# The second column half of a projection, token block by token block, from weights kept in dead tiles

## The chip, the core and the metric

The kernel runs on one core of a Trainium2 chip. The metric is the device time of one execution in microseconds. Shown are the median of several runs, and one profiled execution with its own time.

## The reference

One sequence of 512 tokens with 1024 features passes through two blocks of two layers. In the first block a layer ends twice in a layer norm, each over a sum with a projection:

```python
x = layer_norm(ALPHA * x + mix, ln1_g[l], ln1_b[l])   # mix = merged @ w_o[l]
ffn = conv_ffn(x, ffn_w_up[l], ffn_conv_w[l], ffn_conv_b[l], ffn_w_down[l])
x = layer_norm(ALPHA * x + ffn, ln2_g[l], ln2_b[l])
```

In the second block each layer has three sublayers: a mixer (RG-LRU in the first layer, RWKV-7 in the second), a cross attention into 256 memory tokens, and an MLP of 4096 with a squared ReLU. Each of them reads an RMS norm of `x`, and each result is normed before it is added:

```python
x = x + rms_norm_2(t, g[1])                            # t = mixer(hn) @ w_out (+ b_out)
c = mem_cross_attention(rms_norm_2(x, g[2]), mem_n, c_w_q[i], c_w_kv[i], c_w_o[i])
x = x + rms_norm_2(c, g[3])
m = sqrelu_mlp(rms_norm_2(x, g[4]), m_w_up[i], m_w_down[i])
x = x + rms_norm_2(m, g[5])
```

All of it is float32.

## The kernel before

The 512 tokens are four blocks of 128, t0 to t3. A float32 product is made of three matmuls in a rounded type: each operand is split into a high and a low part, and high x high, high x low and low x high are added in PSUM (`mm3`, and L347 to L349 in `nmm`). A weight unit is 128 x 1024. `W` (L277 to L285) brings it in: a transfer on SP's queue into `wst` (two buffers, L280), the high part by ACT into `whi` (four buffers, L283), the low part by POOL into `wlo` (three buffers, L284). Behind a transposed input of 1024 features a projection to 1024 columns has two column halves of 512, with four units each, and each unit serves two of the eight feature chunks.

A projection whose result has tokens on the partitions goes through `nmm`: four PSUM banks, one for each token block (three under the name `mm`, one under `av`), and for each unit 6 matmuls per block. The argument `tail` says how many of the last units are run block by block: 1 in the first column half; 3 in the second, so that the first unit is run for all blocks, and then t0 has its other 18 matmuls, then t1, and so on. When a block's last matmul is done, `evac` reads its bank and the norm of that block begins; `skew` holds the norms as generators, so that their stages are emitted staggered. The program's order is not the final one: a scheduler in the compiler orders each engine's instructions by what they wait for, and it mixes the blocks.

Nine projections are followed by a norm over their rows. In the order of time: wo0 (`attention`'s end in the first block), wn0 (the FFN's down projection), wo1, wn1, wlo (the RG-LRU's output, with a bias), wco0 (cross attention), wmd0 (MLP down), wco1 and wmd1; RWKV's output has another form and is untouched. In the FFN and the MLP the down projection is summed over groups of chunks; the last group is the one before the norm. The FFN's last group has six chunks, three units for each half, with a tail of two. The MLP's 32 chunks go in groups of 6, 6, 6, 6, 6 and 2, so its last group has one unit for each half.

Behind the last matmul of a block in the second block of the network come (`out_proj`, `post`, `pre_norm`): ACT's square with its sum (L906), VectorE's product with the norm's row (L963; for wlo and the MLP POOL's, L967 and L1154), an inverse root in small VectorE steps (L374 to L380, L911), the pair of L945 that adds the result to `x`, then the next norm: squares (L906), products with its row by POOL and VectorE (L922), the inverse root, and the diagonal `dg` (L926). The transposes at L931 are matmuls of `work` with `dg`, eight for each token block, and ACT (L295) and VectorE (L297) split their result into `xTh` and `xTl`. In the first block of the network `ln_fin` does the same with a layer norm (L414 to L442) and `to_T` transposes (L391). The next stage starts with `lead`: the first output tiles are computed for tokens 0 to 255, as soon as two blocks are transposed, and then for the others. The weights of `lead` are loaded ahead and split by ACT and POOL.

## Time and profile before

| | before |
|---|---|
| median of 3 runs | 3947.04 us (3946.8 to 3949.09) |
| profiled execution | 3947.95 us, span 3946.2 us |
| mean granted clock of TensorE | 0.951 |
| TensorE (PE) busy | 3724.7 us, 94% |
| VectorE (DVE) busy | 1740.0 us, 44% |
| POOL busy | 1639.7 us, 42% |
| ACT busy | 1505.6 us, 38% |
| chain that ended last | PE 81%, DVE 11%, DMA 3% |

The span is what the profile covers; the time of the execution is 1.75 us longer. PE means TensorE's matmuls and PEld its weight loads, which run beside them. A clock of 1.00 is the higher of TensorE's two levels. A busy share is a mean over stages with different limits, so that an engine at 44% can still be what a stage waits for.

### The profile page before, as it was taken

To read this page: it belongs to the slowest core of one execution; us is meant where nothing else is said; L and a number is where in the kernel's file an instruction comes from. 1 tells how busy PE (TensorE), PEld (TensorE's weight loads), DVE (VectorE), ACT (ScalarE), POOL (GpSimd) and SP (SyncE) were. 2 spreads that over 40 slices of the span, in tenths; PEclk is the share of its full clock that TensorE was granted. 3 is DMA by queue.
4 is the path that set the end of the run, shared out by engine and by line. 5 is a ranking of instruction groups with operands and counts; after the bars stand their busy time and mean duration, and the time that the engine had idled before them with its cause. 6 is when DMAs were issued, how large, how long until landed. Compare 5 with 4: busy or idle time off the path is not lost.

```text
span 3946.2 us, 48388 instructions
## 1 busy us (share of the span) xinstructions
PE 3724.7 (94%) x18540; PEld 2992.9 (76%) x18540; DVE 1740.0 (44%) x3587; ACT 1505.6 (38%) x2653; POOL 1639.7 (42%) x876
## 2 busy tenths in 40 slices
PE   8999998999999999989997888999799899798998
PEld 8766777888886677778886777888676677687886
DVE  4553354433545424453437645221468545534113
ACT  4433333433344334333334634332354334343322
POOL 4421436444452233444444562344434322434444
PEclk9999999999999999999998998999899658899999
DMA  5311323333342122232321321222223311322222
GB/s 188 115 54 48 92 61 126 91 99 97 125 150 70 59 72 70 91 111 93 100 92 59 101 102 64 86 96 92 97 75 96 70 39 49 121 80 84 98 91 86
DMA packets 148952, 354.10 MB, mean 90 GB/s; under 512 B 50080, under 2 KB 60864, under 8 KB 148464
## 3 DMA queue, kind: packets, MB, share of 16 engines
q1 hardware_dynamic: 148448, 350.18, 27.4%
q8 instruction: 146, 2.39, 0.2%
q0 software_dynamic: 272, 0.82, 0.1%
q14 instruction: 86, 0.70, 0.1%
HBM read 332.56 MB, written 18.38 MB: 89 GB/s over the span
## 4 chain that ended last, share of the span: by engine, by line
PE 81%; DVE 11%; DMA 3%; ACT 2%; POOL 2%; issue 1%; SPq 0%; DVEq 0%; POOLq 0%; ACTq 0%
PE mm L289 13%; PE mm L291 13%; PE mm L290 13%; PE mm L1626 3%; PE mm L348 3%; PE mm L347 3%; PE mm L349 3%; PE mm L1144 2%; PE mm L1146 2%; PE mm L1145 2%; PE sc L778 2%; PE mm L862 2%; PE mm L861 2%; PE mm L860 2%; PE av L616 1%
## 5 line engine op out<-in xcount | busy, mean ns | idle before, releaser
L284 POOL TENSOR_TENSOR wlo<-wst,whi 128x1024 fp32r<-128x1024 f32 (+1 forms) x556 | 1340.5, 2414 | 1912.2 <-PE mm L291 971.2
L283 ACT ACTIVATE whi<-wst 128x1024 fp32r<-128x1024 f32 (+1 forms) x556 | 582.8, 1048 | 1134.0 <-DMA wst<-in_wmd 143.3
L289 PE MATMUL mm<-xTh,whi 128*128 128x512 f32 (+1 forms) x2208 | 834.2, 380 | 10.6 <-ACT whi L283 10.3
L290 PE MATMUL mm<-xTl,whi 128*128 128x512 f32 (+1 forms) x2208 | 834.5, 379 | 2.3 <-DVE xTl L297 2.1
L291 PE MATMUL mm<-xTh,wlo 128*128 128x512 f32 (+1 forms) x2208 | 833.4, 378 | 0.0
L289 PEld LDWEIGHTS mm<-xTh,whi 128*128 128x128 f32 x2208 | 417.7, 190 | 96.2 <-ACT whi L283 11.7
L291 PEld LDWEIGHTS mm<-xTh,wlo 128*128 128x128 f32 x2208 | 418.2, 190 | 84.3 <-issue 8.7
L290 PEld LDWEIGHTS mm<-xTl,whi 128*128 128x128 f32 x2208 | 418.5, 190 | 83.9 <-issue 7.8
L822 DVE SCALAR_TENSOR_TENSOR fup<-mm,vec,fup 128x511 f32<-128x511 f32 (+1 forms) x176 | 131.6, 748 | 237.5 <-ACT fup L820 234.5
L784 ACT ACTIVATE P<-sc,sm 128x128 f32<-128x128 f32 x192 | 100.7, 525 | 229.5 <-DVE sm L782 229.5
L781 DVE TENSOR_TENSOR sc<-sc,cst 128x128 f32<-128x128 f32 x192 | 56.0, 297 | 277.2 <-PE sc L780 258.5
L1117 DVE TENSOR_TENSOR relu<-relu,mm 128x512 f32<-128x512 f32 x64 | 43.9, 687 | 294.5 <-ACT relu L1116 294.5
L349 PE MATMUL mm<-whi,xTl 128*128 128x512 f32 (+1 forms) x432 | 164.3, 383 | 2.4 <-DVE xTl L297 2.4
L348 PE MATMUL mm<-wlo,xTh 128*128 128x512 f32 (+1 forms) x432 | 165.4, 383 | 0.0
L347 PE MATMUL mm<-whi,xTh 128*128 128x512 f32 (+1 forms) x432 | 161.4, 383 | 2.4 <-ACT zkv L475 1.1
L1144 PE MATMUL mm<-whi,ph 128*128 128x512 f32 x384 | 151.9, 396 | 0.0
L1145 PE MATMUL mm<-wlo,ph 128*128 128x512 f32 x384 | 151.9, 396 | 0.0
L931 PE MATMUL tr<-dg,work 128*128 128x128 f32 x384 | 67.3, 348 | 89.4 <-DVE dg L926 80.0
L1146 PE MATMUL mm<-whi,pl 128*128 128x512 f32 x384 | 150.2, 396 | 0.0
L931 PEld LDWEIGHTS tr<-dg,work 128*128 128x128 f32 x384 | 63.7, 258 | 93.5 <-issue 63.1
L1151 DVE TENSOR_TENSOR work<-work,mm 128x512 f32<-128x512 f32 x60 | 41.2, 687 | 190.1 <-PE mm L1146 190.1
L860 PE MATMUL mm<-whi,hh 128*128 128x512 f32 x264 | 103.6, 392 | 0.0
(554 smaller groups left out, 7184.7 us busy)
## 6 DMA issues: line engine op xcount, KB each, us to landing
wst<-in_wu SPq DMA_DIRECT2D x88, 512.0 KB, 3.6
wst<-in_wmu SPq DMA_DIRECT2D x64, 512.0 KB, 3.6
wst<-in_wmd SPq DMA_DIRECT2D x64, 512.0 KB, 3.6
wst<-in_wg SPq DMA_DIRECT2D x48, 512.0 KB, 3.6
wst<-in_wn SPq DMA_DIRECT2D x44, 512.0 KB, 3.6
wst<-in_wa SPq DMA_DIRECT2D x24, 512.0 KB, 3.6
wst<-in_wb SPq DMA_DIRECT2D x24, 512.0 KB, 3.6
wst<-in_wd SPq DMA_DIRECT2D x24, 512.0 KB, 3.6
```

The lines of the kernel that those rows point to most:

```text
L283: nc.scalar.activation(hi, st, AF.Copy)
L284: nc.gpsimd.tensor_sub(lo, st, hi.bitcast(F32))
L289: mm(out, lh, rh, start=start, stop=False)
L290: mm(out, lh, rl, start=False, stop=False)
L291: return mm(out, ll, rh, start=False, stop=stop)
L347: mm(o, xh, hi[:, s], start=k == 0, stop=False)
L348: mm(o, xh, lo[:, s], start=False, stop=False)
L349: mm(o, xl, hi[:, s], start=False, stop=k == nk - 1)
L860: mm(pss[t], hh[:, ts], wh[:, s], start=j == js[0], stop=False)
L1144: mm(pss[t], hh[:, ts], wh[:, s], start=j == js[0], stop=False)
L1145: mm(pss[t], hh[:, ts], wl[:, s], start=False, stop=False)
L1146: mm(pss[t], hl[:, ts], wh[:, s], start=False, stop=j == js[-1])
```

## The change

In the nine projections the second column half runs one token block after the other: all 24 matmuls of t0 (18 where there are three units), then those of t1, and so on (`tokens`). That needs all units of this half at once. They are loaded during the first half, in turn with its own units (`side` in `nmm`): `W_in` brings a unit through `wst` like `W`, but splits it into tiles that are dead in this stage, under the name `wres`. These are 512 columns wide, so that ACT and POOL have two splits for each unit, except at wco, where two large tiles hold two units each. In the MLP the groups of chunks become 6, 6, 6, 4, 4 and 6, so that its last group has three units for each half. The number of matmuls and of transfers is as before; ACT and POOL have 24 splits more.

```diff
+KEEP = dict(ffn=(["q"] * 4, ["k"] * 2 + ["pt"] * 2, ["tmp"] * 4), mlp=(["q"] * 4, ["k"] * 4, ["tmp"] * 4))
...
+    def W_in(self, name, u, his, los):
+        nc = self.nc
+        st = self.wp.tile([128, 1024], F32, tag="wst", bufs=2, name="wst")
+        nc.sync.dma_start(st, self.I[name][u])
+        w = 1024 // len(his)
+        for i, (hi, lo) in enumerate(zip(his, los)):
+            s = slice(i * w, i * w + w)
+            nc.scalar.activation(hi, st[:, s], AF.Copy)
+            nc.gpsimd.tensor_sub(lo, st[:, s], hi.bitcast(F32))
+        if len(his) == 2:
+            return list(zip(his, los))
+        return [(his[0][:, i * 512:i * 512 + 512], los[0][:, i * 512:i * 512 + 512]) for i in range(2)]
+
+    def halves(self, tags):
+        a = [self.t([128, 512], tag, {"pt": 9, "tmp": 5}.get(tag, 8), F32R, "wres") for tag in tags]
+        return a[:2], a[2:]
+
+    def tokens(self, xT, units, evac, bank="mm"):
+        mm = self.nc.tensor.matmul
+        pss = self.banks(NT)
+        for t in range(NT):
+            ts = slice(t * 128, t * 128 + 128)
+            for k, (hi, lo) in enumerate(units):
+                xh, xl = xT[k][0][:, ts], xT[k][1][:, ts]
+                mm(pss[t], xh, hi, start=k == 0, stop=False)
+                mm(pss[t], xh, lo, start=False, stop=False)
+                mm(pss[t], xl, hi, start=False, stop=k == len(units) - 1)
+            evac(t, pss[t])
...
         for kp in range(nu):
             units.append(self.W(name, u0 + kp))
+            if kp < len(side):
+                side[kp]()
...
-            self.nmm(f"wo{l}", 4 * cb, self.pairs(mT), evo, tail=1 if cb == 0 else 3)
+        self.two_pass(f"wo{l}", self.pairs(mT), evo, [lambda i=i: self.halves(("k" if i < 2 else "pt",) * 4) for i in range(4)])
...
+    def two_pass(self, name, yT, evac, tiles):
+        units = []
+
+        def load(i):
+            units.extend(self.W_in(name, 4 + i, *tiles[i]()))
+        self.nmm(name, 0, yT, lambda t, ps: evac(0, t, ps), side=[lambda i=i: load(i) for i in range(4)])
+        self.tokens(yT, units, lambda t, ps: evac(1, t, ps))
...
-            for cb, ev in todo:
-                self.nmm(name, 4 * cb, yT, ev, tail=1 if cb == 0 else 3)
+            self.two_pass(name, yT, ev, tiles)
...
-        groups = [range(6 * a, min(32, 6 * a + 6)) for a in range(6)]
+        ends = [6, 12, 18, 22, 26, 32]
+        groups = [range(a, b) for a, b in zip([0] + ends, ends)]
...
+                if fin and cb == 1:
+                    self.tokens([hs[j] for j in js], kept, evac)
+                    continue
+                kept = []
+
+                def keep(a):
+                    kept.extend(self.W_in(f"wmd{i}", 16 + js[0] // 2 + a, *self.halves(KEEP["mlp"][a])))
+                self.nmm(f"wmd{i}", cb * 16 + js[0] // 2, [hs[j] for j in js], evac, nk=len(js),
+                         side=[lambda a=a: keep(a) for a in range(nu)] if fin else ())
```

The FFN's last group is written in the same way as the MLP's. In wco the tiles are two of the large ones, in wlo those of the names k, k, pt and q.

The first place where the order moves is TensorE in the second column half of wco0. `mm_18529` to `mm_18531` and `av_18532` are the banks of t0 to t3, `whi_18577` and `wlo_18578` the last unit. Before, near the end of the half:

```order
L347 MATMUL av_18532<-whi_18565,ph_18190 128x512
L348 MATMUL av_18532<-wlo_18566,ph_18190 128x512
L348 MATMUL mm_18529<-wlo_18578,ph_18360 128x512
L349 MATMUL mm_18529<-whi_18577,pl_18361 128x512
L347 MATMUL mm_18529<-whi_18577,ph_18371 128x512
L348 MATMUL mm_18529<-wlo_18578,ph_18371 128x512
L349 MATMUL mm_18529<-whi_18577,pl_18372 128x512
L348 MATMUL mm_18530<-wlo_18578,ph_18360 128x512
L349 MATMUL mm_18530<-whi_18577,pl_18361 128x512
L347 MATMUL mm_18530<-whi_18577,ph_18371 128x512
L348 MATMUL mm_18530<-wlo_18578,ph_18371 128x512
```

Here t3's bank gets matmuls of the second unit while t0 and t1 still lack most of the last. In the changed kernel (the banks are `mm_18619` to `mm_18621` and `av_18622`, the units lie in the two `wres`), at the passage from t0 to t1:

```order
L316 MATMUL mm_18619<-wres_18544,ph_18432 128x512
L317 MATMUL mm_18619<-wres_18544,pl_18433 128x512
L315 MATMUL mm_18619<-wres_18544,ph_18443 128x512
L316 MATMUL mm_18619<-wres_18544,ph_18443 128x512
L317 MATMUL mm_18619<-wres_18544,pl_18444 128x512
L315 MATMUL mm_18620<-wres_18475,ph_18177 128x512
L316 MATMUL mm_18620<-wres_18475,ph_18177 128x512
L317 MATMUL mm_18620<-wres_18475,pl_18178 128x512
L315 MATMUL mm_18620<-wres_18475,ph_18188 128x512
```

The 24 matmuls of t0 stand one behind the other, then the 24 of t1; behind those of t3 come the transposes of t0, those of t1 and the lead.

The second place is POOL at the same time: the splits of the next stage's weights (wmu, of the MLP's up projection) against the multiplications of the second norm (`work` from `x` and `row`, one for each token block). Before, where `wlo_18893`, `wlo_18899` and `wlo_18905` are the next stage's:

```order
L284 TENSOR_TENSOR wlo_18572<-wst_18569,whi_18571 128x1024
L284 TENSOR_TENSOR wlo_18578<-wst_18575,whi_18577 128x1024
L284 TENSOR_TENSOR wlo_18893<-wst_18890,whi_18892 128x1024
L284 TENSOR_TENSOR wlo_18899<-wst_18896,whi_18898 128x1024
L922 TENSOR_TENSOR work_18377<-x_13033,row_18387 128x512
L922 TENSOR_TENSOR work_18379<-x_13034,row_18387 128x512
L284 TENSOR_TENSOR wlo_18905<-wst_18902,whi_18904 128x1024
L922 TENSOR_TENSOR work_18381<-x_13035,row_18387 128x512
L922 TENSOR_TENSOR work_18383<-x_13036,row_18387 128x512
L284 TENSOR_TENSOR wlo_19079<-wst_19076,whi_19078 128x1024
```

In the changed kernel, where `wlo_18959`, `wlo_18965` and `wlo_18971` are the next stage's:

```order
L297 TENSOR_TENSOR wres_18475<-wst_18510,wres_18475 128x1024
L285 TENSOR_TENSOR wlo_18541<-wst_18538,whi_18540 128x1024
L297 TENSOR_TENSOR wres_18544<-wst_18545,wres_18544 128x1024
L297 TENSOR_TENSOR wres_18544<-wst_18579,wres_18544 128x1024
L285 TENSOR_TENSOR wlo_18576<-wst_18573,whi_18575 128x1024
L285 TENSOR_TENSOR wlo_18959<-wst_18956,whi_18958 128x1024
L285 TENSOR_TENSOR wlo_18965<-wst_18962,whi_18964 128x1024
L285 TENSOR_TENSOR wlo_18971<-wst_18968,whi_18970 128x1024
L959 TENSOR_TENSOR work_18449<-x_13061,row_18459 128x512
L959 TENSOR_TENSOR work_18451<-x_13062,row_18459 128x512
L959 TENSOR_TENSOR work_18453<-x_13063,row_18459 128x512
L959 TENSOR_TENSOR work_18455<-x_13064,row_18459 128x512
```

The kept units' splits stand between those of the first half, and all three splits of the next stage stand ahead of the four multiplications.

## Rows read from the trace of the kernel before

**Rows 1.** The page, busy time, share of the span and instructions of each engine.

```profile
PE 3724.7 (94%) x18540; PEld 2992.9 (76%) x18540; DVE 1740.0 (44%) x3587; ACT 1505.6 (38%) x2653; POOL 1639.7 (42%) x876
```

**Rows 2.** Table of waits, PE: us in total, times, longest.

```profile
PE tr L931 <- DVE dg L926: 80.0, 9, 21.0
```

**Rows 3.** Windows: width, busy (count) of PE, PEld, DVE, ACT, POOL, PEclk, DMA share, GB/s.

```profile
671.85:707.50 35.65, 25.77 (x177) 24.56 (x178) 23.08 (x41) 12.79 (x18) 19.57 (x11) 0.76 0.29 88
1050.10:1066.70 16.60, 12.98 (x65) 10.99 (x63) 16.46 (x44) 6.29 (x10) 10.21 (x11) 0.90 0.40 147
1713.66:1749.00 35.34, 24.99 (x178) 23.93 (x178) 23.15 (x41) 12.80 (x18) 19.59 (x11) 0.81 0.29 104
2095.38:2138.10 42.72, 19.93 (x140) 19.65 (x141) 33.48 (x110) 14.36 (x30) 16.27 (x10) 0.68 0.06 19
2299.16:2342.05 42.89, 28.29 (x209) 27.85 (x210) 29.47 (x83) 15.48 (x33) 18.60 (x10) 0.80 0.26 94
2445.79:2487.70 41.91, 28.77 (x209) 28.24 (x210) 29.72 (x85) 16.56 (x35) 16.29 (x8) 0.80 0.21 70
2824.88:2860.29 35.41, 11.21 (x66) 10.63 (x65) 30.78 (x91) 16.22 (x38) 16.34 (x21) 0.70 0.26 90
3554.05:3594.40 40.35, 27.00 (x209) 26.42 (x210) 28.44 (x85) 16.52 (x35) 15.31 (x8) 0.87 0.16 54
3931.61:3946.20 14.59, 0.00 (x0) 0.00 (x0) 10.31 (x36) 0.86 (x4) 2.64 (x3) 0.60 0.36 144
```

**Rows 4.** Windows, the stretch of wco0 in which TensorE stands still.

```profile
2449.79:2457.11 7.32, 0.00 (x0) 0.03 (x1) 7.32 (x34) 4.34 (x10) 4.39 (x3) 0.50 0.24 87
```

**Rows 5.** Windows, work behind wco0 at full clock, and 128x512 matmuls of wco0.

```profile
2471.17:2487.70 16.53, 16.53 (x142) 16.53 (x142) 5.45 (x7) 5.69 (x9) 4.47 (x2) 1.00 0.07 17
...
2424.00:2436.00 12.00, 12.00 (x53) 9.64 (x52) 1.38 (x2) 3.75 (x5) 6.02 (x3) 1.00 0.32 108
```

**Rows 6.** Timeline of ACT in wco0: start, us, instruction, idle before it.

```profile
2439.81 0.60 ACT L906 ACTIVATE junk<-mm 128x512 f32<-128x512 f32 x1 [6.88 <-PE mm L349]
...
2440.98 0.60 ACT L906 ACTIVATE junk<-mm 128x512 f32<-128x512 f32 x1 [0.48 <-PE mm L349]
```

**Rows 7.** Timeline of DVE in wco0.

```profile
2444.09 4.59 DVE L945 SCALAR_TENSOR_TENSOR x<-work,rsq,x 128x512 f32<-128x512 f32 x2
...
2450.52 1.41 DVE L945 SCALAR_TENSOR_TENSOR x<-work,rsq,x 128x512 f32<-128x512 f32 x2
...
2456.68 0.28 DVE L926 TENSOR_SCALAR dg<-cst,rsq 128x128 f32<-128x128 f32 x1
...
2461.76 0.27 DVE L926 TENSOR_SCALAR dg<-cst,rsq 128x128 f32<-128x128 f32 x1
```

**Rows 8.** Timeline of POOL in wco0.

```profile
2442.98 5.15 POOL L284 TENSOR_TENSOR wlo<-wst,whi 128x1024 fp32r<-128x1024 f32 x2 [8.80 <-PE av L349]
```

**Rows 9.** Timeline of DVE at the kernel's end, the last pair.

```profile
3940.58 1.41 DVE L945 SCALAR_TENSOR_TENSOR x<-work,rsq,x 128x512 f32<-128x512 f32 x2
```

**Rows 10.** The page, groups of the splits, and transfers of a weight unit.

```profile
L284 POOL TENSOR_TENSOR wlo<-wst,whi 128x1024 fp32r<-128x1024 f32 (+1 forms) x556 | 1340.5, 2414 | 1912.2 <-PE mm L291 971.2
L283 ACT ACTIVATE whi<-wst 128x1024 fp32r<-128x1024 f32 (+1 forms) x556 | 582.8, 1048 | 1134.0 <-DMA wst<-in_wmd 143.3
...
wst<-in_wmd SPq DMA_DIRECT2D x64, 512.0 KB, 3.6
```

**Rows 11.** Timeline of SP, the issues of wlo's eight transfers.

```profile
2237.50 37.22 SPq L280 DMA_DIRECT2D wst<-in_wlo  x8
```

**Rows 12.** Timeline of DVE in wn1: t0's last addition, the first diagonal.

```profile
2087.02 0.69 DVE L868 TENSOR_TENSOR x<-x,mm 128x512 f32<-128x512 f32 x1 [6.98 <-PE mm L862]
...
2115.94 0.27 DVE L926 TENSOR_SCALAR dg<-cst,rsq 128x128 f32<-128x128 f32 x1
```

**Rows 13.** Timeline of DVE behind wmd0: the last diagonal.

```profile
2852.98 0.29 DVE L926 TENSOR_SCALAR dg<-cst,rsq 128x128 f32<-128x128 f32 x1
```

**Rows 14.** Windows, a stretch of the RWKV stage.

```profile
3160.00:3220.00 60.00, 56.57 (x337) 43.79 (x336) 32.48 (x90) 27.18 (x75) 26.76 (x48) 0.59 0.17 42
```

More of the change, by code (lines that the diff above doesn't have):

```diff
@@ L873, in down, with keep @@
+                if fin and cb == 1:
+                    self.tokens([hs[j] for j in js], kept, evac)
+                    continue
+                kept = []
+                def keep(i):
+                    kept.extend(self.W_in(f"wn{l}", 11 + js[0] // 2 + i, *self.halves(KEEP["ffn"][i])))
+                self.nmm(f"wn{l}", u0, [hs[j] for j in js], evac, nk=len(js),
+                         side=[lambda i=i: keep(i) for i in range(nu)] if fin else ())
             if fin:
@@ L1103, in cross, with tiles @@
         T2 = self.newT()
-        self.out_proj(f"wco{i}", o, x, post_g, pre_g, T2)
+        hold = []
+        def tiles(i):
+            if i % 2 == 0:
+                hold.append(self.big([128, 2, 2, 1024], name="wres"))
+            a = hold[-1][:, i % 2]
+            return [a[:, 0]], [a[:, 1]]
+        self.out_proj(f"wco{i}", o, x, post_g, pre_g, T2, tiles=[lambda i=i: tiles(i) for i in range(4)])
         return self.pairs(T2)
@@ L1132, in down @@
             for cb in range(2):
-                pss = self.banks(NT)
-                units = [self.W(f"wmd{i}", cb * 16 + js[0] // 2 + a) for a in range(nu)]
-                order = [(t, a) for a in range(nu - 1) for t in range(NT)] + [(t, nu - 1) for t in range(NT)]
-                for t, a in order:
-                    wh, wl = units[a]
-                    ts = slice(t * 128, t * 128 + 128)
-                    for kk in range(2):
-                        j = js[2 * a + kk]
-                        s = slice(kk * 512, kk * 512 + 512)
-                        hh, hl = hs[j]
-                        mm = nc.tensor.matmul
-                        mm(pss[t], hh[:, ts], wh[:, s], start=j == js[0], stop=False)
-                        mm(pss[t], hh[:, ts], wl[:, s], start=False, stop=False)
-                        mm(pss[t], hl[:, ts], wh[:, s], start=False, stop=j == js[-1])
-                    if a == nu - 1:
-                        if gi == 0:
-                            nc.scalar.activation(work[t][cb], pss[t], AF.Copy)
-                        else:
-                            nc.vector.tensor_add(work[t][cb], work[t][cb], pss[t])
-                        if fin:
-                            self.square(work[t][cb], ss[t], cb)
-                            nc.gpsimd.tensor_mul(work[t][cb], work[t][cb], gp[:, cb * 512:cb * 512 + 512])
-                        if fin and cb == 1:
-                            self.skew(fin_row(t))
@@ new lines, in evac @@
+                def evac(t, ps, cb=cb):
+                    if gi == 0:
+                        nc.scalar.activation(work[t][cb], ps, AF.Copy)
+                    else:
+                        nc.vector.tensor_add(work[t][cb], work[t][cb], ps)
+                    if fin:
+                        self.square(work[t][cb], ss[t], cb)
+                        nc.gpsimd.tensor_mul(work[t][cb], work[t][cb], gp[:, cb * 512:cb * 512 + 512])
+                    if fin and cb == 1:
+                        self.skew(fin_row(t))
@@ L1157, in down @@
+                if fin and cb == 1:
+                    self.tokens([hs[j] for j in js], kept, evac)
+                    continue
+                kept = []
+                def keep(a):
+                    kept.extend(self.W_in(f"wmd{i}", 16 + js[0] // 2 + a, *self.halves(KEEP["mlp"][a])))
+                self.nmm(f"wmd{i}", cb * 16 + js[0] // 2, [hs[j] for j in js], evac, nk=len(js),
+                         side=[lambda a=a: keep(a) for a in range(nu)] if fin else ())
             if fin:
@@ L1277, in rglru @@
         T2 = self.newT()
-        self.out_proj("wlo", self.pairs(yT), x, ROW_G + 1, ROW_G + 2, T2, bias=ROW_BOUT)
+        self.out_proj("wlo", self.pairs(yT), x, ROW_G + 1, ROW_G + 2, T2, bias=ROW_BOUT,
+                      tiles=[lambda g=g: self.halves(g) for g in (["k"] * 4, ["k"] * 4, ["pt"] * 4, ["q"] * 4)])
         return self.pairs(T2)
```

93 lines of the change are left out of this document (36 added, 57 removed).

## The prediction

> **What bounds the kernel now.** I read the page first: TensorE is busy 3724.7 of 3946.2 us [rows 1], so the kernel is bound by matmuls and can only shorten where TensorE stands still or runs slowly. The table of waits says where it stands: TensorE's largest wait, 80.0 us in nine times, is that of the transposes at L931 for the diagonal `dg` that VectorE writes last in a norm [rows 2]. The third view is the table of windows, one window for each of the nine places where a projection is followed by a norm: from the end of the projection's last matmul (E below) to the point where the next matmuls run without a stop [rows 3]. The nine windows are 305.5 us together, and TensorE is busy in 178.9 us of them. Besides, the granted clock in them is 0.60 to 0.90, and 0.50 in the stretch of wco0 in which TensorE has nothing to do [rows 4]: of the two levels, 1.2 and 2.4 GHz, that is the lower, so the first transposes behind an idle stretch run at half speed.
>
> What would these windows be if nothing waited? After wco0 the work at full clock is 142 instructions in 16.53 us, 0.1164 us each; a 128x512 matmul goes at 53 in 12.00 us, 0.226 us each [rows 5]. Width less count times 0.1164 is a window's excess: wo0 35.65 - 177 x 0.1164 = 15.0; wo1 14.6; wn1 26.4; wlo 18.6; wco0 17.6; wmd0 27.7; wco1 16.0; wmd1, the kernel's end, 14.6. In wn0 many of the 65 instructions are wider, so there I take the idle 3.6 and a tenth of the busy 12.98 for the clock, 5. The sum is 155: the most that this change can win, were everything behind it free.
>
> Why the wait is so long is seen at wco0. The four token blocks are nearly finished together: ACT's first squares of t0 and t1 start at 2439.81 and 2440.98, when their matmuls are done, 6.0 and 4.8 us ahead of E = 2445.79 [rows 6]. VectorE then serves four blocks at once: the diagonals of t0 and t1 come at 2456.68 and 2461.76, 16.9 and 20.8 us behind those ends [rows 7]. In that time POOL splits weights of the next stage, two in 5.15 us from 2442.98 [rows 8], and VectorE's pair of L945 takes 4.59 us, against 1.41 us a little later [rows 7].
>
> **The change, part by part.** No matmul goes or comes. In the second column half a token block runs its 24 matmuls (18 at wn and wmd) without a break. At 0.226 us that is 5.4 us (4.1), so t0 is finished at E - 16.3, t1 at E - 10.9, t2 at E - 5.4 (E - 12.2, - 8.1, - 4.1). E itself stays where it was if the weights come in time.
>
> *Four places alike (wo0, wo1, wco0, wco1).* t0 is finished 10 us and t1 6 us earlier against E. Their chains keep the same instructions, but two blocks share VectorE where four did. How long one then takes no row shows. The nearest row from below is the kernel's end, where the last block's chain ends 10.4 us behind E, 3941.99 against 3931.61, though without the second norm [rows 9]; from above, 16.9 and 20.8 as now. I take the middle, 13.5 for t0 and 16 for t1. So t0's diagonal is there before E and t1's at E + 5.1, with t0's eight transposes, 0.9 us, to run meanwhile: 4 us stay. TensorE's pause is then too short for most of the loss by clock. The gains are 11.0, 10.6, 13.6 and 12.0, together 47.2. The bounds are 6 each (t1's shift alone, chains as long as now) and the whole excess.
>
> *wlo.* As wco0, with a bias addition more in the chain: 5 us stay. But here the supply costs something. A unit takes its buffer through a transfer (3.6), ACT's split (1.05) and POOL's (2.41) [rows 10], 7.1 us; with two buffers one unit every 3.5 us. The first half now needs eight units, 28 us, where its matmuls take 96 x 0.226 = 21.7. If nothing is loaded ahead, the price is 28 - 21.7 = 6.5 us. wlo's transfers are issued from 2237.50 on [rows 11], and its first matmul runs some 192 x 0.226 = 43 us before E = 2299.16, at 2256: a lead of 18 us, which the two buffers and the three sets of split tiles can't hold in full. I put 4 us of the 6.5. At the other four places of this size the transfers stand in SP's order ahead of the last work of the stage before, which covers them; I cost them at nothing, and 6.5 each if that cover is gone. Gain 18.6 - 9 = 9.6.
>
> *wn0.* 5 to 2: gain 3.
>
> *wn1.* t0's last addition starts at 2087.02, 8.4 us before E = 2095.38, and the first diagonal comes at 2115.94 [rows 12]; VectorE is busy 33.48 of 42.72 us there [rows 3]. So the bounds are 12.2 - 7.7 = 4.5 (t0's earlier end) and VectorE's idle 9.2. I take 7.
>
> *wmd0.* Blocks are now 1.4 us apart, and the next stage needs all four: t3's diagonal comes at 2852.98, 28.1 us behind E, for VectorE is busy 30.78 of 35.41 with all four [rows 3, 13]. In the change t0's chain and most of t1's run before E, and t3 queues behind one block: about 10.4 and one more norm, 14. Gain 14, bounds 4 (half of t0's 8.1 us shift) and 18.
>
> *wmd1.* The last block alone: E + 10.4 becomes about E + 6, and the output's transfer of 4.2 us stays. Gain 4.5, bounds 2 and 6.
>
> *Groups of chunks in the MLP.* There are six groups as before, so as many additions and as many matmuls; the last, of six chunks instead of two, gives the blocks their 18 matmuls. Cost nothing. *Splits:* ACT and POOL get 24 instructions more, each over half a width, beside matmuls. *Order:* the scheduler also moves RWKV steps against each other. There the clock is 0.59 in a stretch with TensorE busy 56.57 of 60 us [rows 14], so that TensorE, not a wait, sets the pace. I count it at nothing; one such stretch at full clock instead of half, or the reverse, is 30 us, and I take that as the bound either way.
>
> **Sum.** 47.2 + 9.6 + 3 + 7 + 14 + 4.5 = 85.3. The profiled execution took 3947.95 us, 0.9 above the median of 3947.04; 3947.95 - 85.3 = 3862.6, less 0.9 is **3862 us**.
>
> **The rule that speaks against it.** VectorE's pair at 4.59 us ran beside POOL's splits, and at 1.41 without them [rows 7, 8]. In the order of the change all three splits for the next stage stand ahead of POOL's four multiplications of the norm; I expect them to run before t0's L945, while t0's matmuls run. If they fall on it instead, each place but the last pays 4.59 - 1.41 = 3.2 us again, up to 8 x 3.2 = 25 us less gain: 3887. The Trainium skill, page SBUF — State Buffer, section Who interferes with whom, says that a VectorE instruction with two SBUF inputs contends with a GpSimd instruction that reads SBUF, and that for the shared ports whoever issues first blocks the other; L945 reads `work` and `x`, so by that rule the new splits would stretch it wherever they overlap, and the time would be that of this case. The trace agrees that the pair is stretched; which splits meet it in the new order no run here shows yet.
>
> **The rivals.**
> - *Chains as long as now* (VectorE's and POOL's queues set the time, not the blocks' ends). For: VectorE is busy 7.32 of 7.32 us while TensorE stands still in wco0 [rows 4], and for 87% of wmd0's window [rows 3]. Against: its work can start up to 10 us earlier, when it is idle. Gains: 4 x 6 + wlo 2 + wn0 1 + wn1 4.5 + wmd0 4 + wmd1 2 = 37.5, so 3909.
> - *All is covered, and the clock stays high.* Gains: the four whole (63.2), wlo 14, wn0 5, wn1 12, wmd0 16, wmd1 6 = 116, so 3831.
> - *Collisions with the splits,* as above: 3887.
> - *RWKV in another order loses* 30 us: 3892.
> - *Slower: the supply.* If the kept units starve the first halves everywhere, five places lose 6.5 us and the four of three units 21 - 16.3 = 4.9 each: 52 us. With the forecast's gains that is still faster, 3914; with chains as long as now it is 3947.95 + 52 - 37.5 - 0.9 = 3961. It decides where less than 6.5 us of supply are ahead at the first matmul. For: each unit passes two buffers. Against: POOL's row in the page waits 971.2 us for TensorE to release buffers [rows 10], so the supply runs ahead most of the time.
> - *The change doesn't do what it says:* the order shows 24 matmuls of one block behind one another, so I give it nothing.
>
> **How the numbers follow.** Chances: forecast 0.57, chains as long as now 0.17, all covered 0.10, collisions 0.08, RWKV 0.05, supply 0.03. The range goes from the case with everything covered to that with chains as long as now, 3831 to 3909; outside stay the supply and the tails of both ends. About 0.2%, 8 us, is what a measurement can tell from no change. Every case but the supply is faster by far more than that: faster 0.95, same 0.02, slower 0.03.
>
> **What would show it.** Right: the wait for `dg` at the transposes falls from 80 to some 30 us; the windows of wo and wco shrink to about 25 us with clocks above 0.9; ACT's first square of t0 starts some 16 us before E. Wrong: TensorE waiting for `wres` or `whi` inside a first column half (supply); L945 pairs of over 4 us (collisions); an unchanged wait of t1's transposes (chains); a different width of the RWKV stage.

## The result, and the profile after

The changed kernel takes 3905.22 us in the median of four runs (3898.12 to 3910.22), against 3946.92 us before: a ratio of 0.9894 with a 95% interval from 0.988 to 0.9909, so 42 us less (36 to 47). Run again on another chip, beside other versions, it gave 0.9884 (0.9857 to 0.991). The forecast was 3862, a gain of 85. The profiled execution took 3908.79 us, with a span of 3907.0; the sums below go by its span, 39.2 us shorter than before.

TensorE's share has risen, as the page's line on the engines shows [rows 1]:

```profile
PE 3738.4 (96%) x18540; PEld 3000.4 (77%) x18540; DVE 1753.8 (45%) x3587; ACT 1507.1 (39%) x2677; POOL 1642.4 (42%) x900
```

The table of waits (PE; us in total, times, longest) no longer has one wait of 80.0 us [rows 2]. The transposes behind the norms, now at L968, wait for the diagonal or for steps of the inverse root next to it, 46.9 us together. Before, these two were 80.0 and 6.8 us, 86.8 together. The wait for POOL's low parts has risen from 5.3 to 12.4 us. Before:

```profile
PE tr L931 <- DVE rsq L380: 6.8, 2, 4.7
PE mm L348 <- POOL wlo L284: 5.3, 5, 1.7
```

After:

```profile
PE tr L968 <- DVE rsq L416: 16.0, 2, 13.9
PE tr L968 <- DVE dg L963: 16.0, 5, 4.3
PE tr L968 <- DVE rsq L412: 14.9, 4, 7.3
PE mm L384 <- POOL wlo L285: 12.4, 11, 1.8
```

The nine windows after, each from the end of the projection's last matmul to the point at which TensorE has done the work that it had done at the end of the same window before [rows 3] (width; busy time and count of PE, PEld, DVE, ACT, POOL; PEclk; DMA share; GB/s):

```profile
678.29:704.43 26.14, 22.32 (x170) 21.44 (x168) 14.97 (x37) 7.76 (x12) 7.76 (x5) 0.93 0.14 46
1051.88:1062.43 10.55, 9.48 (x58) 8.56 (x57) 10.41 (x28) 3.00 (x5) 3.94 (x8) 1.00 0.28 107
1716.59:1744.61 28.02, 23.68 (x169) 22.61 (x170) 15.71 (x40) 7.78 (x12) 7.78 (x5) 0.88 0.22 63
2092.18:2129.82 37.64, 20.24 (x141) 19.96 (x141) 27.57 (x108) 12.70 (x26) 12.41 (x8) 0.73 0.01 1
2295.88:2329.62 33.74, 27.88 (x209) 27.72 (x209) 21.23 (x69) 12.56 (x27) 10.36 (x7) 0.90 0.18 67
2434.61:2462.58 27.97, 25.17 (x209) 24.59 (x209) 18.22 (x50) 11.29 (x23) 6.96 (x4) 1.00 0.06 21
2799.35:2825.78 26.43, 11.28 (x65) 10.68 (x64) 21.79 (x78) 13.52 (x32) 10.90 (x17) 0.81 0.23 82
3530.74:3558.65 27.91, 25.16 (x210) 24.59 (x209) 18.16 (x50) 11.29 (x23) 6.93 (x4) 1.00 0.01 2
3895.45:3906.99 11.54, 0.00 (x1) 0.00 (x0) 6.81 (x17) 0.72 (x2) 1.26 (x1) 0.66 0.26 104
```

They are 229.9 us together, against 305.5 us: 75.5 us less. So the windows gave most of what was forecast, and 36.3 us of it were given back elsewhere. Place by place:

| place | excess before | forecast gain in the window | measured |
|---|---|---|---|
| wo0, wo1 | 15.0, 14.6 | 11.0, 10.6 | 9.5, 7.3 |
| wn0 | 5 | 3 | 6.1 |
| wn1 | 26.4 | 7 | 5.1 |
| wlo | 18.6 | 13.6 | 9.1 |
| wco0, wco1 | 17.6, 16.0 | 13.6, 12.0 | 13.9, 12.4 |
| wmd0 | 27.7 | 14 | 9.0 |
| wmd1 (the end) | 14.6 | 4.5 | 3.0 |
| sum | 155 | 89.3 | 75.5 |

To see what was given back, and where, I laid the traces against each other by the work that TensorE had done (0.233 us for each 512 columns, 0.117 for a transpose) and read the times of equal work. Of the 36.3 us, 12.1 lie in the RWKV stage. The first halves of wo0, wo1 and wlo cost 2.4, 3.6 and 4.6 us, that of wn0 some 3.4 (by run 11 below) and wn1 1.4. In wo0, wo1 and wn0 t0's eight transposes, 0.9 us each time, now lie ahead of the window and are no gain. The two attentions took 4.4 us longer with the same waits as before: behind three pauses that stand in both kernels the granted clock fell in this execution and not in that of before. In the 12 us from 390, 588 and 1428 us it is 0.86; before, in the 12 us from 390, 588 and 1431, it is 1.00. The rest is 1.7.

**The RWKV stage.** Between the points at 2680 and 2920 us of TensorE work the same 2912 matmuls run in both kernels, on which the change edits nothing. The windows of that stretch, before and after (columns as above):

```profile
2951.43:3423.92 472.49, 422.75 (x2912) 332.05 (x2911) 277.60 (x688) 188.66 (x472) 169.55 (x188) 0.77 0.27 77
```

```profile
2916.13:3400.75 484.62, 437.18 (x2912) 342.44 (x2911) 283.86 (x693) 189.15 (x474) 174.48 (x189) 0.74 0.27 76
```

TensorE stands still for 49.7 us in the one and 47.4 in the other, so the 12.1 us are no new wait: its busy time has risen by 14.4 us, at a granted clock of 0.74 instead of 0.77.

**wo's first half.** SP's queue issues, in the stretch in which the last units of wo0 are due, a block of `x`, two rows of the layer norm and two weight units (start, duration of the issue):

```profile
638.28 0.33 SPq L764 DMA_DIRECT2D x<-in_x  x1
638.66 0.90 SPq L273 DMA_DIRECT2D row<-in_rows  x2
639.67 0.36 SPq L281 DMA_DIRECT2D wst<-in_wo  x1
640.68 0.33 SPq L292 DMA_DIRECT2D wst<-in_wo  x1
```

Five transfers move at the same time, and ACT's split of the unit issued at 639.67 starts only when it has landed, 7.2 us later (idle 8.41 us before it):

```profile
646.85 1.06 ACT L284 ACTIVATE whi<-wst 128x1024 fp32r<-128x1024 f32 x1 [8.41 <-DMA wst<-in_wo]
```

TensorE's waits in that place, of which the second and the fourth are this unit's:

```profile
PE tr L427 <- DVE xTl L330: 2.6, 1, 2.6
PE mm L384 <- POOL wlo L285: 1.3, 1, 1.3
PE mm L322 <- ACT xTh L328: 1.0, 1, 1.0
PE mm L383 <- ACT whi L284: 0.5, 1, 0.5
```

**wn0's first half** shows that a short stall can cost more than its length. TensorE waits 1.30 us for a low part of POOL, which now has the kept units' splits in its queue:

```profile
1028.22 0.50 PE L384 MATMUL mm<-wlo,hh 128*128 128x512 f32 x1 [1.30 <-POOL wlo L285]
```

In the 4 us behind it the clock is 0.58, and 10 matmuls run where some 17 would at full clock:

```profile
1028.00:1032.00 4.00, 3.78 (x10) 2.97 (x11) 1.38 (x2) 0.37 (x1) 2.63 (x3) 0.58 0.44 116
1032.00:1042.00 10.00, 10.00 (x46) 8.24 (x45) 6.78 (x17) 3.25 (x4) 5.62 (x3) 1.00 0.35 118
```

**The chains.** At wco0 the diagonals of t0 and t1 come at 2431.90 and 2437.97, that is 14.1 and 14.6 us behind their blocks' last matmuls (E = 2434.61 less 16.8 and 11.2, the time of the 72 and 48 matmuls of later blocks). Before, 16.9 and 20.8 us were counted from ACT's first squares [rows 6, 7]; counted from there, it is 13.3 and 14.5 us now. The two squares and the two diagonals:

```profile
2418.63 0.58 ACT L943 ACTIVATE junk<-mm 128x512 f32<-128x512 f32 x1
...
2423.50 0.60 ACT L943 ACTIVATE junk<-mm 128x512 f32<-128x512 f32 x1 [4.20 <-PE mm L317]
...
2431.90 0.27 DVE L963 TENSOR_SCALAR dg<-cst,rsq 128x128 f32<-128x128 f32 x1
...
2437.97 0.27 DVE L963 TENSOR_SCALAR dg<-cst,rsq 128x128 f32<-128x128 f32 x1
```

At wlo (E = 2295.88) they are 17.6 and 20.1 us late, and the diagonal of t3 comes at E + 18.2. VectorE in that place, one half of t0's pair at L982 and the four diagonals:

```profile
2284.30 2.60 DVE L982 SCALAR_TENSOR_TENSOR x<-work,rsq,x 128x512 f32<-128x512 f32 x1
...
2297.03 1.16 DVE L963 TENSOR_SCALAR dg<-cst,rsq 128x128 f32<-128x128 f32 x1
...
2304.96 0.28 DVE L963 TENSOR_SCALAR dg<-cst,rsq 128x128 f32<-128x128 f32 x1
...
2311.99 0.28 DVE L963 TENSOR_SCALAR dg<-cst,rsq 128x128 f32<-128x128 f32 x1
...
2314.11 0.29 DVE L963 TENSOR_SCALAR dg<-cst,rsq 128x128 f32<-128x128 f32 x1
```

### The profile page after: what moved, and what is told of

Same layout as the page of the kernel before. It is cut to its first block, busy times and chain, and to the rows that moved or that the text cites. A ratio compares the mean times of both kernels' runs of the same rounds, so it can differ in the third digit from the quotient of the medians.

```text
span 3907.0 us, 48377 instructions
## 1 busy us (share of the span) xinstructions
PE 3738.4 (96%) x18540; PEld 3000.4 (77%) x18540; DVE 1753.8 (45%) x3587; ACT 1507.1 (39%) x2677; POOL 1642.4 (42%) x900
## 4 chain that ended last, share of the span: by engine, by line
PE 76%; DVE 9%; DMA 5%; POOL 4%; ACT 3%; issue 3%; SPq 0%; POOLq 0%; DVEq 0%; ACTq 0%
PE mm L322 13%; PE mm L323 13%; PE mm L324 13%; PE mm L384 5%; PE mm L383 5%; PE mm L385 5%; PE mm L1665 4%; POOL wlo L285 2%; PE av L383 2%; PE av L385 2%; PE av L384 2%; PE sc L823 2%; PE av L652 1%; PE tr L843 1%; ACT whi L284 1%
## 5 line engine op out<-in xcount | busy, mean ns | idle before, releaser
L285 POOL TENSOR_TENSOR wlo<-wst,whi 128x1024 fp32r<-128x1024 f32 (+2 forms) x524 | 1260.2, 2408 | 1784.2 <-PE mm L324 900.9
L284 ACT ACTIVATE whi<-wst 128x1024 fp32r<-128x1024 f32 (+2 forms) x524 | 548.7, 1048 | 1100.0 <-DMA wst<-in_wu 153.1
L867 DVE SCALAR_TENSOR_TENSOR fup<-mm,vec,fup 128x510 f32<-128x510 f32 (+1 forms) x176 | 131.0, 747 | 220.1 <-ACT fup L865 217.1
L384 PE MATMUL mm<-wlo,xTh 128*128 128x512 f32 (+1 forms) x360 | 137.4, 382 | 5.2 <-POOL wlo L285 5.2
L385 PE MATMUL mm<-whi,xTl 128*128 128x512 f32 (+1 forms) x360 | 136.4, 380 | 0.0
L383 PE MATMUL mm<-whi,xTh 128*128 128x512 f32 (+1 forms) x360 | 132.8, 382 | 3.6 <-ACT whi L284 3.6
L968 PE MATMUL tr<-dg,work 128*128 128x128 f32 x384 | 61.9, 328 | 46.9 <-DVE rsq L416 16.0
L297 POOL TENSOR_TENSOR wres<-wst,wres 128x512 fp32r<-128x512 f32 (+1 forms) x56 | 83.7, 1512 | 37.1 <-ACT wres L296 32.2
L968 PEld LDWEIGHTS tr<-dg,work 128*128 128x128 f32 x384 | 58.8, 240 | 50.3 <-issue 33.6
```

Source lines behind the costliest of these rows:

```text
L284: nc.scalar.activation(hi, st, AF.Copy)
L285: nc.gpsimd.tensor_sub(lo, st, hi.bitcast(F32))
L383: mm(o, xh, hi[:, s], start=k == 0, stop=False)
L384: mm(o, xh, lo[:, s], start=False, stop=False)
L385: mm(o, xl, hi[:, s], start=False, stop=k == nk - 1)
L867: nc.vector.scalar_tensor_tensor(a[:, d:], ps[:, :512 - d], self.v(f"fc{l}{tap}", o + j), a[:, d:], op0=OP.mult, op1=OP.add)
```

## The experiments

Each was timed beside the kernel before on the same chip; ratios are against it. "Stage" is the RWKV stretch above, by the time between the points of equal work.

**1. The MLP as before.** `mlp` is put back, with groups of 6, 6, 6, 6, 6 and 2.

```diff
-        ends = [6, 12, 18, 22, 26, 32]
-        groups = [range(a, b) for a, b in zip([0] + ends, ends)]
+        groups = [range(6 * a, min(32, 6 * a + 6)) for a in range(6)]
...
-                    self.tokens([hs[j] for j in js], kept, evac)
```

> The MLP's groups and its down projection as before the change; everything else as in the changed kernel. In the changed kernel the stretches behind wmd0 and at the kernel's end are 10.0 and 3.5 us shorter than before, and the RWKV stage (the TensorE work between 2640 and 2920 us of full-clock work) is 12.2 us longer, 526.6 against 514.5. Theory A (the RWKV stage got longer because the scheduler ordered it otherwise, and the order here is again nearly that of before): both gains are lost and the RWKV loss too, so about 3905 + 13.5 - 12 = 3907, RWKV stage about 514. Theory B (its length is a matter of when the clock falls in an execution, whatever the order): 3905 + 13.5 = 3918, RWKV stage anywhere from 510 to 530.

Ratio 0.992 (0.9889 to 0.995), 3919.94 us. wmd0's place gains 2.7 us against before instead of 10.2, and the end nothing: the MLP's new last group is worth 10 us. The stage is 482.8 us. Its order on TensorE is near that of before, yet the loss stays. The single runs lie between 3904 and 3934 us, at mean clocks of 0.962 to 0.952, which speaks for theory B.

**2. wo as before.**

```diff
-        self.two_pass(f"wo{l}", self.pairs(mT), evo, [lambda i=i: self.halves(("k" if i < 2 else "pt",) * 4) for i in range(4)])
+            self.nmm(f"wo{l}", 4 * cb, self.pairs(mT), evo, tail=1 if cb == 0 else 3)
```

> The two attention output projections (wo0, wo1) as before; everything else as in the changed kernel. Theory A (the gain at wo is real but mostly given back in the first half by a stall of 2.4 to 3.6 us and by transposes that now lie ahead of the end): the two places lose 4.5 and 2.5 us of gain, about 3912. Theory B (the kept units cost as much as the order wins): within 2 us of the changed kernel. The RWKV order differs again here; its stage is compared by itself.

Ratio 0.9922 (0.9907 to 0.9937), 3919.63 us. wo0 and wo1 are within 0.6 us of before, so the change's 5.9 and 2.5 us there are real, theory A; the stage took 494.4 us, the longest of all, at a clock of 0.75.

**3. The layer norm's rows later.**

```diff
-        g, b = self.row(4 * l), self.row(4 * l + 1)
+        gb = []
...
         def evo(cb, t, ps):
+            if cb == 1 and t == 0:
+                gb.extend((self.row(4 * l), self.row(4 * l + 1)))
```

> At wo0 and wo1 the two rows of the layer norm (512 KB each on the queue) are requested behind the kept units instead of ahead of the last two units; everything else as in the changed kernel, the order of the RWKV stage too. Theory A (the last units of wo land late, 7.2 us after their issue against 3.6, because the rows and a block of x are moved in the same moment): TensorE's stall before the last sixth of the first half (0.5 and 1.3 us in wo0, 1.7 and 1.3 in wo1, 2.4 and 3.6 us by the work done) goes, about 3905 - 6 = 3899. Theory B (two buffers for eight units are too few whatever else is moved): the stall stays, 3905.

Ratio 0.9883 (0.9866 to 0.9899), 3904.07 us. TensorE's waits in wo0 have lost both lines that the units caused:

```profile
PE tr L427 <- DVE xTl L330: 2.6, 1, 2.6
PE mm L322 <- ACT xTh L328: 1.5, 1, 1.5
```

By equal work the first halves of wo0 and wo1 now cost 0.0 us against 2.4 and 3.6: theory A. As a whole the run is within its interval of the changed kernel.

**4. Products on VectorE.**

```diff
-                nc.gpsimd.tensor_mul(work[t][cb], work[t][cb], gp[:, s])
+                (nc.gpsimd if cb == 0 else nc.vector).tensor_mul(work[t][cb], work[t][cb], gp[:, s])
```

> The second half's product with the norm's row at wlo and at both MLPs' last groups is made by VectorE instead of POOL (12 products in all); everything else as in the changed kernel. Theory A (t0's and t1's chains wait there for POOL, whose product stands behind a split of the next stage's weights: the second of t0's L982 pair started 2 us late at wlo and at wmd0): each of these windows gets 2 to 4 us shorter, the end 1 us, about 3898 apart from the RWKV stage. Theory B (VectorE's own queue bounds the chains, 0.7 us more for each product): windows as long as now or up to 2 us longer.

Ratio 0.9866 (0.9851 to 0.9881), 3897.89 us, which looks like a gain, though the intervals overlap; but wlo's place and wmd0's are within 0.7 us of the changed kernel, and t0's and t1's diagonals at wlo come 17.6 and 20.0 us behind their blocks, as without the edit. Theory B. What is shorter is the stage, 472.0 us.

**5. The changed kernel again.** No edit.

> The changed kernel itself once more, beside the three that follow, to have its time on the same chip and a second profile of it. Theory A (the RWKV stage differs from one execution to the next, because the clock falls at other moments): its RWKV stage (TensorE work from 2680 to 2920 us) is not again 484.6 us but anywhere from 472 to 494, while the stretches behind the nine places agree with the first profile within 1 us. Theory B (the order of the instructions sets it): 484 again, within 2 us.

Ratio 0.9884 (0.9857 to 0.991), 3905.55 us. The stage took 476.0 us, with the very order of the first profile: 8.6 us of the 12.1 were the clock's chance in that execution. Eight of the nine places agree within 1.2 us; wo1, with its first half, differs by 2.8. There the waits in the first half are nearly alike (1.7 and 1.3 us in the first profile, 1.3 and 1.3 here), but here the clock fell behind them, to 0.66 in the 10 us from 1684, and stayed at 1.00 in the window, which is 22.7 us long; in the first profile it was the other way round, and the window took 28.0 us at a clock of 0.88.

**6. Kept units in the old order.** In `tokens` the first unit is run for all blocks, then the others block by block.

```diff
-        for t in range(NT):
+        todo = [(t, 0) for t in range(NT)] + [(t, 1) for t in range(NT)]
+        for t, part in todo:
...
+                if (k < 2) != (part == 0):
+                    continue
```

> The kept units stay, but the second half runs the first unit for all four blocks and only then block by block, as before the change. So t0 and t1 finish at E - 12.6 and E - 8.4 instead of E - 16.8 and E - 11.2 in the places of four units, and at E - 8.2 and E - 5.5 instead of E - 12.2 and E - 8.2 in those of three. Theory A (what counts is how early the first two blocks are finished; the chains behind them are as long): each place loses the shift of t1, 2.8 us (2.7), and wmd0 and the end less: 8 x 2.7, about 20 us slower than the changed kernel. Theory B (it is enough that the units are there and the scheduler no longer mixes the blocks; the chains wait for VectorE and POOL anyway): within 5 us of the changed kernel.

Ratio 0.9909 (0.9891 to 0.9927), 3916.1 us: 10.5 us slower than the changed kernel beside it. Beside run 5, wco0 and wco1 win 7.4 and 6.2 instead of 12.8 and 12.4 us, wmd0 6.4 instead of 10.6, wn0 and wn1 lose 5 and 2.5, wlo's window is only 0.7 us longer; but wo0 and wo1 win 4 and 3 us more. The windows of wo0 and wo1 in this run:

```profile
676.49:698.98 22.49, 21.14 (x169) 20.12 (x170) 15.31 (x35) 6.61 (x10) 6.75 (x4) 1.00 0.18 52
1714.27:1736.80 22.53, 21.17 (x169) 20.14 (x170) 15.34 (x35) 6.61 (x10) 6.77 (x4) 1.00 0.26 76
```

and wo1's in run 5:

```profile
1718.08:1740.79 22.71, 20.76 (x169) 19.88 (x168) 13.29 (x29) 6.55 (x10) 6.63 (x5) 1.00 0.26 75
```

TensorE idles 1.4 us in each window of run 6, where it idled 3.8 and 4.3 in the first profile of the block order and 4.2 and 2.0 in run 5: t2's transposes wait 0.7 and 0.8 us for VectorE to empty their bank, where they waited 2.6, and 1.5 in the last of these four. The rest is the clock, 1.00 in both windows here; at wo1 the 3 us against run 5 lie in the first half, where run 5's clock fell. Theory A holds for wco, wn and wmd0, and falls for wo and nearly for wlo.

**7. Oldest block first.**

```diff
-            self.open = [c for c in self.open[::-1] if next(c, self) is not self][::-1]
+            self.open = [c for c in self.open if next(c, self) is not self]
```

> The norms' generators are advanced oldest block first instead of newest first, so that VectorE's order has t0's second inverse root and diagonal ahead of t1's pair of additions; nothing else differs from the changed kernel. Theory A (the chains of wlo, wn1, wmd0 stay long because VectorE, which works in order, has the long instructions of the next block between the small steps of the first one's inverse root): t0's and t1's diagonals come 3 us earlier in each place (wlo: from 17.6 and 20.1 us behind their blocks to about 14.5 and 16), and the windows shrink by 2 to 4 us each, some 15 us in all, apart from the RWKV stage. Theory B (VectorE is simply busy, and what one block wins the next one loses): the windows as long as now.

Ratio 0.9817 (0.9801 to 0.9833), 3879.26 us: 26 us faster than the changed kernel. The diagonals of wlo (its E is 2291.50):

```profile
2289.87 0.28 DVE L963 TENSOR_SCALAR dg<-cst,rsq 128x128 f32<-128x128 f32 x1
...
2298.11 0.87 DVE L963 TENSOR_SCALAR dg<-cst,rsq 128x128 f32<-128x128 f32 x1
...
2306.46 0.28 DVE L963 TENSOR_SCALAR dg<-cst,rsq 128x128 f32<-128x128 f32 x1
...
2314.12 0.28 DVE L963 TENSOR_SCALAR dg<-cst,rsq 128x128 f32<-128x128 f32 x1
```

t0's and t1's come 14.9 and 17.6 us behind their blocks, 2.7 and 2.5 us earlier, nearly as theory A has it; but t3's comes at E + 22.6 instead of E + 18.2, and wlo's place wins nothing more. wn1 and wmd0 are within 2 us too; only wco0 and wco1 win 1.4 us each or more. So theory B for the places: where VectorE serves four blocks almost without a pause (here it is busy 20.6 of the 22.6 us from E to t3's diagonal), what the first blocks win the last loses. The 26 us are mainly the stage, 461.3 us at a clock of 0.81, 14.7 less than in run 5:

```profile
2912.42:3373.69 461.27, 405.00 (x2912) 318.25 (x2911) 279.26 (x695) 188.14 (x474) 176.23 (x189) 0.81 0.28 80
```

**8. Both, oldest first and late rows.**

> The last edit together with the late rows at wo0 and wo1. Theory A: both gains add, since they lie in different places (wo's first half; the windows behind the nine places): some 20 us below the changed kernel. Theory B (at wo the kept units' transfers, not the rows, set the pace): no more than the edit of the order alone.

Ratio 0.9807 (0.9791 to 0.9823), 3875.05 us. The intervals of runs 7 and 8 overlap, but the places show that both gains stay: wo0 and wo1 win 8.7 and 6.2 us. The stage has the order of run 7 and took 465.3 us.

**9. The kernel before, oldest first.** The edit of run 7 alone.

> The kernel before, with the norms' generators advanced oldest block first; token-by-token halves, kept units and groups as before the change. In the changed kernel this edit took 26 us, of which the profile puts only some 4 into the nine stretches and 15 into the RWKV stage (461 us against 476 to 485), where nothing of the edit lies. Theory A (the RWKV gain is the scheduler's other order of that stage, and any edit ahead of it may give or take as much): here the nine stretches move by less than 2 us each, and the RWKV stage by something between -15 and +15 us from 472.5. Theory B (the edit itself shortens RWKV's own norms and what waits for them): the RWKV stage again 11 to 15 us shorter, about 458, so about 3947 - 15 = 3932 on the scale of the first chip.

Ratio 1.0022 (1.001 to 1.0034), 3957.7 us: slower by 0.2%. The stage took 478.6 us, 6 longer than before, in an order of its own. Theory B falls: oldest first doesn't shorten RWKV as such.

**10. Two Newton steps instead of three,** on top of run 8. It leaves out the third step of the inverse root in each norm that uses `rs1`, so its arithmetic differs from that of the kernels.

```diff
-        for _ in range(3):
+        for _ in range(2):
```

> The version with the oldest block first and the late rows, and each inverse root of a norm with two Newton steps instead of three: two VectorE instructions less in each of the eight roots behind a projection (about 0.45 us a root, 3.6 us a place). Theory A (behind wlo, wn1 and wmd0 VectorE's work on four blocks is the bound, so that earlier first blocks only move the wait to the last one): these three stretches get about 3 us shorter each, wco and wo 1 to 2, about 3875 - 14 = 3861 apart from the RWKV stage. Theory B (the waits are for POOL and ACT, whose work is the same): less than 1 us each.

Ratio 0.9785 (0.9769 to 0.9801), 3864.17 us. Against run 8 wlo with its first half is 3.2 us shorter, wn1 2.1, wmd0 1.7, wco 1.0 each: at wlo nearly the 3.6 us of VectorE that each place saves. Theory A there, less clearly at wn1 and wmd0.

**11. Kept units two units later,** on top of run 8.

```diff
-            if kp < len(side):
-                side[kp]()
+            if side and kp >= 2:
+                side[kp - 2]()
...
+        for f in side[nu - 2:] if side else ():
+            f()
```

> The version with the oldest block first and the late rows, and the kept units lag by two: the transfers go W0, W1, W2, K0, W3, K1, K2, K3 instead of W0, K0, W1, K1 and so on. Theory A (in wlo the first half's last unit is late by 4.5 us only because three kept units go ahead of it through the two buffers): wlo's first half gets 4 us shorter, those of wn0 and wn1 1 us, and the kept units still come in time, since the second half needs its fourth unit only 4 us after it starts: about 3875 - 6 = 3869 apart from the RWKV stage. Theory B (eight units through two buffers take as long in any order): the stall moves to the start of the second half, the same time.

Ratio 0.9842 (0.9822 to 0.9861), 3884.91 us. wlo's first half costs 0.2 instead of 5.1 us, and wn0 and wn1 win 3.4 and 4.1 us more than in run 8: theory A. But wlo's window gives most of it back, run 8's first and then this one's:

```profile
2288.01:2321.87 33.86, 27.33 (x210) 26.79 (x209) 23.39 (x67) 11.23 (x25) 10.75 (x7) 0.90 0.18 64
```

```profile
2277.89:2315.67 37.78, 29.16 (x210) 28.55 (x210) 27.14 (x84) 12.14 (x27) 11.68 (x7) 0.86 0.16 59
```

So the place wins 1.0 us in all, near theory B, though not by a stall for the kept units. The transfers of the next stage (wcq) follow behind the kept ones; one of ACT's splits waits for such a unit, t0's square stands behind that split, and VectorE, which waits for the square, is idle for 6.76 us, against 1.57 at this step in run 8:

```profile
2267.19 1.06 ACT L284 ACTIVATE whi<-wst 128x1024 fp32r<-128x1024 f32 x1 [3.02 <-DMA wst<-in_wcq]
...
2268.90 0.21 DVE L952 TENSOR_SCALAR rsq<-ss 128x1 f32<-128x1 f32 x1 [6.76 <-ACT junk L947]
```

The time as a whole is worse: the stage took 486.4 us in yet another order, and wo0 loses 2.5.

**12 and 13. The same at wn0, wn1 and wlo alone,** on top of runs 8 and 10. On TensorE the stage's order is that of run 7 and of run 10, instruction for instruction.

> The version with the oldest block first and the late rows, and the kept units lag by two at wn0, wn1 and wlo alone. TensorE's order of the RWKV stage is instruction for instruction that of the two runs with the oldest block first (461.3 and 465.3 us there). Theory A (the order of that stage sets its time, within some 4 us): RWKV stage 458 to 470; wn0 and wn1 win what they won when all units lagged (3.4 and 5.6 us), wlo 1.7, wo keeps its gain: 3875 - 10 = 3865. Theory B (when the clock falls is chance, or hangs on all that ran before): RWKV stage anywhere from 460 to 490, so 3865 to 3890.

> The same with two Newton steps in each inverse root of a norm. Its RWKV order is instruction for instruction that of the earlier run with two steps (469.3 us). Theory A: RWKV stage 465 to 474 and the same gains ahead of it, 3864 - 10 = 3854. Theory B: RWKV stage from 460 to 490, so 3845 to 3875.

Run 12: ratio 0.9786 (0.977 to 0.9802), 3865.23 us, and the stage 462.3 us:

```profile
2899.05:3361.33 462.28, 409.40 (x2912) 322.11 (x2911) 278.46 (x695) 187.96 (x474) 177.33 (x189) 0.80 0.28 79
```

Run 13: 0.9772 (0.9754 to 0.9791), 3858.18 us, but the stage 477.6 us, outside what theory A allowed, and single runs from 3850 to 3866. Run 12 keeps the arithmetic of the kernels and is some 40 us faster than the changed kernel; the interval of run 13 overlaps it.

The stage by its order on TensorE (run 0 is the changed kernel's profile of the result):

| order of | us in each profile |
|---|---|
| before | 472.5 |
| the change (runs 0, 5, 3) | 484.6, 476.0, 478.8 |
| runs 1, 6 | 482.8, 477.5 |
| runs 7, 8, 12 | 461.3, 465.3, 462.3 |
| runs 10, 13 | 469.3, 477.6 |
| runs 2; 4; 9; 11 | 494.4; 472.0; 478.6; 486.4 |

One order varies by up to 8.6 us, the orders by 33. So both theories hold in part. That the order sets a level is shown for the order of runs 7, 8 and 12 against that of the change, whose values lie apart; chance adds some 4 us either way, and of an order that was profiled once, that of the kernel before too, no more than one value is known.

## Why the forecast was half wrong

**Right.** It is faster, and the mechanism is the one described. The windows gave 75.5 of the forecast 89.3 us (85.3 and the 4 us that wlo's supply was to cost). wco, from which the argument was made, came as worked out: 13.9 and 12.4 us for 13.6 and 12.0, with chains of 14.1 and 14.6 us where 13.5 and 16 were taken and the first pause behind E gone. wlo's supply cost 4.6 us for 4 in the first half, its last units late as said; but run 11 shows that without it the place would have won only 1.0 us more. RWKV stayed inside its bound of 30. That 3905 us lies near the 3909 of the rival of chains as long as now is a coincidence: at wco they got shorter, and run 6 shows that the blocks' ends count there. The signs named ahead came only in part. ACT's first square of t0 at wco0 starts 16.0 us before E, as said. The wait of the transposes fell from 80.0 (86.8 with the steps of the root) to 46.9 us, not to 30, and the windows of wo and wco to 26.1, 28.0, 28.0 and 27.9 us, not to 25, at clocks of 0.93, 0.88, 1.00 and 1.00 where above 0.9 was said.

**Sums and readings.** The prices of 6.5 and 4.9 us for the supply come out with 3.53 us for a unit; with the 28 and 21 us as they are printed it would be 6.3 and 4.7. The slower rival counts wlo's 4 us twice. wn1's lower bound takes t0's end 7.7 us before E, where the row has its addition start 8.4 us before E, so 3.8 instead of 4.5. None of this moves the forecast.

**Wrong, step by step.**

*"I cost them at nothing" (the supply at the other four places), and wn without a word of it.* wco had the cover, wo hadn't: it cost 2.4 and 3.6 us. It was not the 6.5 us rate of two buffers but five transfers at once, since SP's order puts `x` and the rows just ahead of the last units; run 3 removes it with the rows. At wn0 and wn1, to which I gave the supply only in the slower rival, runs 11 and 12 win 3.4 and 3.3 us, and 4.1 in both, by loading the kept units later. With t0's transposes (2.7 us) the first halves of wo and wn gave back some 13 us.

*wmd0, "t3 queues behind one block: about 10.4 and one more norm, 14".* t3's diagonal came at E + 19.3 (E = 2799.35), since it still queues behind most of three blocks, t0's own diagonal coming only at E + 6.9: 9.0 us instead of 14. VectorE is busy 21.79 of that window's 26.43 us.

```profile
2806.24 0.27 DVE L963 TENSOR_SCALAR dg<-cst,rsq 128x128 f32<-128x128 f32 x1
...
2818.69 0.29 DVE L963 TENSOR_SCALAR dg<-cst,rsq 128x128 f32<-128x128 f32 x1
```

Likewise wlo 9.1 for 13.6. I had taken VectorE's queue as the bound only at wn1, where 5.1 came for 7; run 10 shows the same bound at wlo, and run 7 that a better order doesn't move it.

*wmd1, "E + 10.4 becomes about E + 6".* It became E + 7.4, from E = 3895.45 to the end of the last pair at 3902.80: 3.0 us for 4.5.

```profile
3901.38 1.42 DVE L982 SCALAR_TENSOR_TENSOR x<-work,rsq,x 128x512 f32<-128x512 f32 x2
```

*wo, "TensorE's pause is then too short for most of the loss by clock".* 9.5 and 7.3 us for 11.0 and 10.6. The idle time in the windows, 3.8 and 4.3 us, is the size of the 4 us that were to stay, though the longer pause is another: t2's transposes wait 2.6 us for VectorE to empty their bank; in run 6, with the blocks less far apart, it is 0.7 and 0.8 us and the windows 22.5. But behind these pauses the clock fell, to means of 0.93 and 0.88, and TensorE's busy time was 22.32 and 23.68 us for 21.14 and 21.17 in run 6, so 1.2 and 2.5 us that the sum put at nothing. In wo1 of run 5, where the pause was 1.5 us and the clock 1.00, the window won 12.6. It is partly chance: at wco0 the same pause of 2.6 us left the clock at 1.00 in the first profile, and in run 5 the window's mean was 0.94.

*RWKV "at nothing".* The middle was wrong: with this change's order the stage took 3.5, 6.3 and 12.1 us more in three profiles than in the one of the kernel before. An estimate of the usual loss, from the spans less the stage (3422.4 and 3424.1 us in runs 0 and 5, 3473.7 before) and the medians, is some 8 us. The order of run 7 was 11 us below the kernel before.

**Collisions.** They were expected to go, and did, but for one place. At wlo a split of the next stage runs on POOL from 2283.90 for 2.44 us,

```profile
2283.90 2.44 POOL L285 TENSOR_TENSOR wlo<-wst,whi 128x1024 fp32r<-128x1024 f32 x1
```

and half a pair of t0, begun at 2284.30, ends 0.6 us behind it, after 2.60 us instead of 0.70. The Trainium skill, page SBUF — State Buffer, section Who interferes with whom, says that the one that issues first blocks the other; these two rows agree. Of four such halves of 2.6 to 2.8 us at wlo and wco before, it is the one left.

**Left open.** Why one order of the RWKV stage keeps the clock at 0.80 and another at 0.75 wasn't tried; only that the stage's idle time goes from 45 to 58 us while its busy time goes from 405 to 437 us.

## What to carry to other kernels

Give an engine's first consumers a head start only where the engine between them has time to use it: at wco the head start became gain, while behind wlo, wn1 and wmd0 VectorE's work on four blocks set the end, so that part of it was lost, an order that favours the first blocks gave at most 2 us more, and less work helped by 1.7 to 3.2. What loads the head start needs must be looked up in the queue's order, transfer by transfer, since one burst of unrelated transfers ahead of the last unit cost 2.4 and 3.6 us here. And a unit that comes earlier can make another later, as at wlo in run 11. And where a scheduler orders the whole program, time the untouched stages too: here the RWKV stage moved by -11 to +22 us from edits that lay elsewhere, more than most of the edits were worth in their own places.

## What was not expected of the hardware

A pause of 1.30 us in wn0 was followed by 4 us at a clock of 0.58. But it needn't be: in the first attention, from 390 to 402 us, the same pause of 1.42 us stands in both kernels, and the clock was 1.00 in the one execution and 0.86 in the other. No edit is near. Run 5, the changed kernel again, has 0.86 there once more; but in the 12 us behind 587 us, where the first profile had 0.86 from 588 on, it has 1.00. And the single runs of one kernel (run 1) spread over 30 us at mean clocks from 0.952 to 0.962, where the kernel before, beside it, spreads over 10.
